# A two-layer decoder trunk: x enters transposed, TensorE multiplies zeros during the first loads, and the attention's compressed branch takes one multiply

## The chip, the cores and the metric

The kernel runs on one core of one Trainium2 chip, one execution per launch. The metric is the device time of one execution in microseconds. The engines of the core are called by the profile's names: PE (TensorE's multiplies; PEld are its weight loads), DVE (VectorE), ACT (ScalarE), POOL (GpSimd) and SP, whose queue issues most DMAs.

## What is computed

Two pre-norm residual layers over 512 positions of 1024 channels, all in float32, then a final RMSNorm. A layer runs two token mixers on one input projection (chunkwise retention, and sparse attention with compressed, selected and window branches), merges them, and adds a SwiGLU FFN of width 2816. Cut to what matters here:

```python
for i in range(2):
    h = rms_norm(x, norm_mix_g[i])               # x: (1, 512, 1024)
    proj = h @ w_in[i]                           # one projection for all branches
    q_r, k_r, v_r, g_r, q_n, kv_n, gate_n, m_a, m_b = split(proj)
    y_ret = (silu(g_r) * group_norm(retention(q_r, k_r, v_r))) @ w_o_ret[i]
    # nsa: kc, vc = compress(blocks of 32 keys/values, stride 16), an MLP with gelu
    # out = g0*softmax(q kc)vc + g1*softmax(selected) + g2*softmax(window)
    y_nsa = nsa(q_n, kv_n, gates, ...) @ w_o_nsa[i]
    x = x + (sigmoid(m_a) * y_ret + sigmoid(m_b) * y_nsa) @ w_out[i]
    x = x + (silu(a) * b) @ w_ffn_out[i]         # a, b = rms_norm(x) @ w_ffn_in[i]
return rms_norm(x, norm_final_g)
```

## The kernel before, in words

Activations are kept transposed, channels on the 128 partitions: x is eight tiles `xt` of 128 x 512. Every float32 product is made of three multiplies in a reduced format (`mm3`, lines 119 to 124): each operand is cut into a high part, a copy by ScalarE, and a low part, the residue by VectorE (`split`, line 78, for weights; `split_scaled`, line 82, for the activations `hh` and `hl`, which carry the norm's gain). A weight of 1 MB is loaded raw (`raw`, three buffers `wr`) and cut into tiles `wh` and `wl` of 1024 columns (`cut`, three buffers each). The norm's factor per position is not applied to the activations but later, to the products: `norm_stats` makes the factor `rstd`, `norm_bcast` spreads it over the partitions as `rb`.

The program is written once with tiles; a planner orders the instructions of each engine by priority (the order in which the code issues them) and by its own estimate of when inputs are ready, and adds the waits. Each engine and each DMA queue then runs its list in order. `issue_after` keeps an instruction behind another one of the same engine in that list.

Before layer 0, `setup` loads x in its natural layout (eight tiles `xnat`) and seven pieces of parameters as rows, then `setup_bias` multiplies the table of relative biases by a one-hot matrix and writes the result to DRAM (`bv`), from which eight strips per layer are loaded with shifted rows. `start_x` transposes x on PE (line 259), copies it (line 262), makes `hh` and `hl`, stores it to `xs` for the residual of layer 0, and sums the squares on VectorE (line 256).

`nsa_kv` begins each layer: the projection `psc` for the compression (48 multiplies of 512 columns), the statistics, the two key halves `psk` (24 multiplies each), the compression of keys and of values (`compress`, a generator of three steps: inputs `z`, `xa` and their cut; 2 x 16 multiplies in line 377; the gelu), the first query projection `q0` in eighteen steps, of which nine stand between two steps of the values' compression, and the values `vs` (96 multiplies of 304 columns). After it the heads run, interleaved with gate projections: scores (lines 530 to 542), transposes of the probabilities (line 573), values (lines 565, 566) and `nsa_finish` (line 588), which adds the compressed branch with two multiplies per head: the same `vc` with the high and the low half of the probabilities of a quad of heads, `pc`. Retention, output projections and FFN follow. The broadcast also stands in `hidden` (lines 871, 872), before the FFN's first products are used.

Of the kernel before, what the change touches and what calls it, by code (L numbers as in the profile page):

```python
# [14 lines left out]
P = 128  # L15
T = 512
# [15 lines left out]
class Builder:  # L32
# [100 lines left out]
    def setup(self):  # L133
        nc, a = self.nc, self.a
        self.bv = self.dr.tile([HN, 640], F32, tag="bv", name="bv")
        self.ident = self.const("ident", [P, P])
        nc.gpsimd.dma_start(self.ident, a["c_ident"])
        rows = self.u("rows", w=P)

        def load_rows():  # L140
            for l in range(DEPTH):
                nc.sync.dma_start(rows[l * 8 : l * 8 + 8], a["norm_mix_g"][l].rearrange("(k p) -> k p", p=P))
                nc.sync.dma_start(rows[16 + l * 8 : 24 + l * 8], a["norm_ffn_g"][l].rearrange("(k p) -> k p", p=P))
            nc.sync.dma_start(rows[32:40], a["norm_final_g"].rearrange("(k p) -> k p", p=P))
            nc.sync.dma_start(rows[40:72], a["cmp_pos_k"].rearrange("l (r q) d -> (l r) (q d)", q=2))
            nc.sync.dma_start(rows[72:104], a["cmp_pos_v"].rearrange("l (r q) d -> (l r) (q d)", q=2))

        self.xnat = []
        for hf in range(2):
            for t in range(NT):  # L150
                xt = self.u("xnat")
                nc.sync.dma_start(xt, a["x"][0, t * P : (t + 1) * P, hf * 512 : (hf + 1) * 512])
                self.xnat.append(xt)
            if hf == 0:
                load_rows()
        self.setup_bias()
        ps = self.tp()
        nc.tensor.transpose(ps[:, :104], rows[:104, :], self.ident[:104, :104])
        self.cols = self.const("cols", [P, 104])
        nc.vector.tensor_copy(self.cols, ps[:, :104])  # L160
# [3 lines left out]
                    "v": [self.cols[:, 72 + l * 16 : 88 + l * 16] for l in range(DEPTH)]}  # L164
        self.mhalf = self.const("mhalf", [P, NT])
# [7 lines left out]
        for g in range(2):  # L173
            nc.vector.memset(self.kcz[g].bitcast(F32), 0.0)
        self.xs = self.dr.tile([KD, P, T], F32, tag="xs", name="xs")
# [6 lines left out]
    def setup_bias(self):  # L182
# [3 lines left out]
        nc.scalar.dma_start(tab[:32], a["rel_bias"])  # L186
        nc.vector.memset(tab[32:33], NEG)
        ohv = self.u("ohv", w=256)
        nc.scalar.dma_start(ohv[:33], a["c_ohv"])
        ps = self.mm()  # L190
# [35 lines left out]
    def norm_stats(self, acc=None, ss=None):  # L226
# [8 lines left out]
        self.last_rstd = nc.gpsimd.tensor_tensor(self.rstd, var, self.mhalf, ALU.pow)  # L235

    def norm_bcast(self):
# [5 lines left out]
        for t in range(NT):  # L243
            nc.tensor.matmul(ps[:, t * P : (t + 1) * P], rep[:, t * P : (t + 1) * P], self.ident, start=True, stop=True)
        nc.scalar.activation(self.rb, ps, AF.Copy)

    def start_x(self):
        nc = self.nc
        h = []
        ss = self.small("ss", 2 * NT)  # L250
        for k in range(KD):
            if k % 4 == 0:
                for t in range(NT):
                    junk = self.u("junk")
                    xn = self.xnat[k + t]
                    nc.vector.tensor_tensor_reduce(junk, xn, xn, 1.0, 0.0, ALU.mult, ALU.add, ss[:, k + t : k + t + 1])
            ps = self.mm() if k % 2 else self.tp()
            for t in range(NT):
# [785 lines left out]
```

## Time and profile before

| | us |
|---|---|
| median of three runs | 2456.5 (2456.14 to 2457.05) |
| the profiled execution | 2455.72 |
| its span, first to last instruction | 2453.9 |
| PE busy, share of the span | 2404.7, 98% |
| DVE, ACT, POOL busy | 1409.4, 1025.3, 252.2 |
| DMA | 262.47 MB, mean 107 GB/s |

A row of a timeline gives the start and the duration of an instruction, or of several alike merged, in microseconds from the span's start; what stands in square brackets is how long the engine was idle before it and what ended that. Multiplies overlap in their records, so the pace of PE is read from the distance of two starts, not from one duration. The granted clock is the share of 2.4 GHz that TensorE was given; where nothing was recorded, the view prints 1.00, and that is so for the first 27 us.

### The profile page before, as it was taken

What the parts mean: (1) busy time and instruction counts of PE and PEld (TensorE: products, weight loads), DVE (VectorE), ACT (ScalarE), POOL (GpSimd) and SP (SyncE); (2) the same over time, 40 slices, a digit from 0 to 9 for tenths busy, and PEclk for the clock granted to TensorE, in tenths of its full rate; (3) what the DMA queues carried; (4) which work ended last, traced back from release to release, by engine and by line L of the source; (5) the groups of instructions that cost most, each with busy time, mean ns of one, the idle gap of its engine ahead of it and who ended that gap; (6) DMA issues with size and microseconds to landing.
All of it is one profiled execution on the core that took longest, in us unless ns stands there. A gap on an engine that the chain in (4) does not pass through costs nothing.

```text
span 2453.9 us, 29372 instructions
## 1 busy us (share of the span) xinstructions
PE 2404.7 (98%) x11115; PEld 1956.1 (80%) x11115; DVE 1409.4 (57%) x2797; ACT 1025.3 (42%) x1862; POOL 252.2 (10%) x225
## 2 busy tenths in 40 slices
PE   7999999999999999999989999999999999999998
PEld 5877777888888878888878787778888877888887
DVE  6778886454574633333567878864545654434334
ACT  4666675233333432222346676642333333222222
POOL 1000000010020110110110000001100202101010
PEclk9999999999999999999999999999999999999999
DMA  7523224522342432323454322235223434223221
GB/s 230 149 74 87 74 69 102 165 85 96 98 142 95 155 102 87 103 87 99 128 141 120 94 79 73 74 102 156 90 93 106 159 110 139 86 86 103 86 95 60
DMA packets 234874, 262.47 MB, mean 107 GB/s; under 512 B 42276, under 2 KB 178637, under 8 KB 234733
## 3 DMA queue, kind: packets, MB, share of 16 engines
q1 hardware_dynamic: 220720, 236.93, 32.0%
q10 hardware_dynamic: 13244, 21.41, 2.4%
q8 instruction: 87, 1.43, 0.2%
q0 software_dynamic: 768, 2.27, 0.2%
q14 instruction: 55, 0.44, 0.1%
HBM read 235.36 MB, written 25.21 MB: 106 GB/s over the span
## 4 chain that ended last, share of the span: by engine, by line
PE 89%; DVE 6%; ACT 3%; issue 1%; POOL 1%; DMA 0%; SPq 0%; POOLq 0%; ACTq 0%; DVEq 0%
PE f L123 12%; PE f L122 12%; PE f L124 12%; PE a L124 8%; PE a L123 7%; PE a L122 7%; PE o L124 7%; PE o L122 7%; PE o L123 7%; PE t L573 2%; DVE p L553 1%; PE o L566 1%; PE o L565 1%; PE a L541 1%; PE a L542 1%
## 5 line engine op out<-in xcount | busy, mean ns | idle before, releaser
L79 ACT ACTIVATE wh<-wr 128x1024 fp32r<-128x1024 f32 (+3 forms) x406 | 397.2, 980 | 986.2 <-PE f L123 263.6
L80 DVE TENSOR_TENSOR wl<-wr,wh 128x1024 fp32r<-128x1024 f32 (+3 forms) x406 | 462.7, 1143 | 220.7 <-ACT wh L79 211.9
L122 PE MATMUL f<-hh,wh 128*128 128x512 f32 x936 | 373.4, 400 | 0.7 <-ACT wh L79 0.5
L124 PE MATMUL f<-hh,wl 128*128 128x512 f32 x936 | 371.5, 397 | 1.8 <-DVE wl L80 1.7
L123 PE MATMUL f<-hl,wh 128*128 128x512 f32 x936 | 370.7, 396 | 0.1
L124 PEld LDWEIGHTS f<-hh,wl 128*128 128x128 f32 x936 | 176.7, 189 | 44.0 <-DVE wl L80 4.1
L122 PEld LDWEIGHTS f<-hh,wh 128*128 128x128 f32 x936 | 176.9, 189 | 36.4 <-ACT wh L79 1.4
L123 PEld LDWEIGHTS f<-hl,wh 128*128 128x128 f32 x936 | 176.8, 189 | 33.9 <-DVE hl L84 0.6
L523 ACT ACTIVATE p<-p,nmx 128x512 f32<-128x512 f32 (+3 forms) x256 | 142.3, 556 | 67.1 <-DVE nmx L522 65.0
L80 DVE TENSOR_TENSOR pt<-t,pt 128x512 fp32r<-128x512 f32 (+3 forms) x256 | 123.5, 485 | 56.2 <-ACT pt L79 54.6
L124 PE MATMUL a<-hh,wl 128*128 128x512 f32 x360 | 144.7, 402 | 9.3 <-DVE wl L80 9.3
L122 PE MATMUL a<-hh,wh 128*128 128x512 f32 x360 | 144.8, 402 | 0.0
L123 PE MATMUL a<-hl,wh 128*128 128x512 f32 x360 | 144.5, 401 | 0.0
L79 ACT ACTIVATE pt<-t 128x512 fp32r<-128x512 f32 (+3 forms) x256 | 109.3, 429 | 71.8 <-PE t L573 66.9
L876 POOL TENSOR_TENSOR fa<-fa,rb 128x512 f32<-128x512 f32 x44 | 77.2, 1755 | 570.1 <-ACT fa L875 570.1
L522 DVE CUSTOM_DVE_ANT_0 p<-a,strip 128x512 f32<-128x512 f32 (+3 forms) x256 | 119.5, 484 | 18.1 <-PE a L542 11.5
L122 PE MATMUL o<-hh,wh 128*128 128x512 f32 x304 | 120.1, 395 | 0.0
L124 PE MATMUL o<-hh,wl 128*128 128x512 f32 x304 | 120.0, 395 | 0.0
L123 PE MATMUL o<-hl,wh 128*128 128x512 f32 x304 | 119.9, 395 | 0.0
L573 PE MATMUL t<-ident,p 128*128 128x128 f32 x640 | 113.7, 273 | 0.0
L573 PEld LDWEIGHTS t<-ident,p 128*128 128x128 f32 x640 | 81.3, 141 | 24.3 <-issue 2.2
L565 PE MATMUL o<-pt,vs 128*128 128x512 f32 (+3 forms) x256 | 91.4, 360 | 1.4 <-ACT pt L79 1.4
(423 smaller groups left out, 4859.4 us busy)
## 6 DMA issues: line engine op xcount, KB each, us to landing
wr<-in_w_in SPq DMA_DIRECT2D x66, 1024.0 KB, 5.3
wr<-in_w_ffn_in SPq DMA_DIRECT2D x44, 1024.0 KB, 5.2
wr<-in_w_ffn_out SPq DMA_DIRECT2D x18, 1024.0 KB, 5.0
wr<-in_w_o_ret SPq DMA_DIRECT2D x16, 1024.0 KB, 5.0
wr<-in_w_in SPq DMA_DIRECT2D x36, 256.0 KB, 4.0
strip<-bv SPq DMA_DIRECT2D x32, 256.0 KB, 5.1
gs<-mt ACTq DMA_DIRECT2D x32, 256.0 KB, 2.0
wr<-in_w_o_nsa SPq DMA_DIRECT2D x16, 512.0 KB, 7.3
```

What stands on the lines that cost most here:

```text
L79: self.nc.scalar.activation(hi, src, AF.Copy)
L80: (eng or self.nc.vector).tensor_sub(lo, src, hi.bitcast(F32))
L122: self.nc.tensor.matmul(ps, lh, rh, start=start and i == 0, stop=False)
L123: self.nc.tensor.matmul(ps, lh, rl, start=False, stop=False)
L124: self.nc.tensor.matmul(ps, ll, rh, start=False, stop=stop and i == n - 1)
L522: nc.vector.tensor_tensor_reduce(p, src, self.backwards(strip, w - 1, w), -1.0, BIG, ALU.add, ALU.min, nmx[:, c])
L523: nc.scalar.activation(p, p, AF.Exp, scale=-1.0, bias=nmx[:, c], accum_out=sm[:, c])
L541: nc.tensor.matmul(ps[:, :w], qh[:, ts], ks[:, br, :w], start=True, stop=False)
L542: nc.tensor.matmul(ps[:, :w], ql[:, ts], ks[:, br, :w], start=False, stop=True)
L565: nc.tensor.matmul(po[:, j * P :], lhs, th, start=br == 0 and j == 0, stop=False)
L573: nc.tensor.transpose(pt[:, (i - j) * P : (i - j + 1) * P], pr[br][i][:, j * P : (j + 1) * P], self.ident)
L876: nc.gpsimd.tensor_mul(t, t, self.rb)
```

## The change

- The host hands over x transposed (`c_xt`) and the parameters as one 128 x 104 array of columns (`c_cols`). `setup` loads the columns; `start_x` loads two tiles of x, then the first 1 MB of `w_in`, then the other six tiles. The transposes, their copies, the sums on VectorE and the stores to `xs` are gone. `mix` of layer 0 reads the residual from `c_xt`.
- The squares of x are made by ScalarE and added by GpSimd (`acc_sq`), and `norm_stats` sums over partitions by multiplies with `ones`, as the other norms do.
- The loads for the bias table move from ScalarE's queue to GpSimd's; its multiply and its stores (`bias_rows`) move behind the first projection.
- PE issues 32 multiplies of a cleared tile, 224 columns each, at the beginning; nothing reads them.
- The statistics are in two parts: in `nsa_kv` the broadcast stands between the two key halves, and the second half is cut and multiplied ahead of the compression. The query steps are placed anew among the compression's. The broadcast is a transpose instead of a multiply by the identity.
- `vc` is one tile for both groups; `pc` holds the high half of two heads and the low half of the same two on the other 64 partitions, so that `nsa_finish` issues one multiply per head.

```diff
     def setup(self):
...
-        self.ident = self.const("ident", [P, P])
-        nc.gpsimd.dma_start(self.ident, a["c_ident"])
-        rows = self.u("rows", w=P)
...
-        self.xnat = []
-        for hf in range(2):
-            for t in range(NT):
-                xt = self.u("xnat")
-                nc.sync.dma_start(xt, a["x"][0, t * P : (t + 1) * P, hf * 512 : (hf + 1) * 512])
-                self.xnat.append(xt)
-            if hf == 0:
-                load_rows()
-        self.setup_bias()
-        ps = self.tp()
-        nc.tensor.transpose(ps[:, :104], rows[:104, :], self.ident[:104, :104])
         self.cols = self.const("cols", [P, 104])
-        nc.vector.tensor_copy(self.cols, ps[:, :104])
+        nc.sync.dma_start(self.cols, a["c_cols"])
         self.gmix = [self.cols[:, l * 8 : l * 8 + 8] for l in range(DEPTH)]
         self.gffn = [self.cols[:, 16 + l * 8 : 24 + l * 8] for l in range(DEPTH)]
...
+        self.ident = self.const("ident", [P, P])
+        nc.gpsimd.dma_start(self.ident, a["c_ident"])
+        self.setup_bias()
...
         self.kcz = [self.const(f"kcz{g}", [P, 224], F32R) for g in range(2)]
         for g in range(2):
             nc.vector.memset(self.kcz[g].bitcast(F32), 0.0)
+
+        ps = self.tp()
+        for _ in range(IDLE):
+            nc.tensor.matmul(ps[:, :224], self.kcz[0][:, :P], self.kcz[1], start=True, stop=True)
...
         nc, a = self.nc, self.a
         tab = self.u("tab", w=HN)
-        nc.scalar.dma_start(tab[:32], a["rel_bias"])
+        nc.gpsimd.dma_start(tab[:32], a["rel_bias"])
         nc.vector.memset(tab[32:33], NEG)
         ohv = self.u("ohv", w=256)
-        nc.scalar.dma_start(ohv[:33], a["c_ohv"])
-        ps = self.mm()
+        nc.gpsimd.dma_start(ohv[:33], a["c_ohv"])
+        self.bias_in = tab, ohv
+
+    def bias_rows(self):
+        nc = self.nc
+        tab, ohv = self.bias_in
+        ps = self.tp()
         nc.tensor.matmul(ps[:HN, :256], tab[:33], ohv[:33], start=True, stop=True)
...
     def norm_bcast(self):
...
         ps = self.tp()
         for t in range(NT):
-            nc.tensor.matmul(ps[:, t * P : (t + 1) * P], rep[:, t * P : (t + 1) * P], self.ident, start=True, stop=True)
+            nc.tensor.transpose(ps[:, t * P : (t + 1) * P], rep[:, t * P : (t + 1) * P], self.ident)
         nc.scalar.activation(self.rb, ps, AF.Copy)
...
     def start_x(self):
-        nc = self.nc
-        h = []
-        ss = self.small("ss", 2 * NT)
-        for k in range(KD):
-            if k % 4 == 0:
-                for t in range(NT):
-                    junk = self.u("junk")
-                    xn = self.xnat[k + t]
-                    nc.vector.tensor_tensor_reduce(junk, xn, xn, 1.0, 0.0, ALU.mult, ALU.add, ss[:, k + t : k + t + 1])
-            ps = self.mm() if k % 2 else self.tp()
...
-                nc.tensor.transpose(ps[:, t * P : (t + 1) * P], self.xnat[4 * (k // 4) + t][:, (k % 4) * P : (k % 4 + 1) * P],
-                                    self.ident)
-            xt = self.u("xt")
-            nc.scalar.activation(xt, ps, AF.Copy)
-            h.append(self.make_h(xt, self.gmix[0][:, k : k + 1]))
-            if k == 2:
-                self.first_h = self.last_hi
-            nc.gpsimd.dma_start(self.xs[k], xt)
+
+        nc = self.nc
+        xts = [self.u("xt") for _ in range(KD)]
+        w = self.a["w_in"][0][:, C_KV : C_KV + 256].rearrange("(k p) n -> p k n", p=P)
+        for k in range(2):
+            last = nc.sync.dma_start(xts[k], self.a["c_xt"][k])
+        with self.tc.issue_after(last.ins):
+            raw = self.raw([(lambda v: v, w)], KD, 256)
+        with self.tc.issue_after(self.last_load.ins):
+            for k in range(2, KD):
+                self.last_x = nc.sync.dma_start(xts[k], self.a["c_xt"][k])
+        h = [self.make_h(xts[k], self.gmix[0][:, k : k + 1]) for k in range(2)]
+        with self.tc.issue_after(self.last_hi.ins):
+            self.first_w = [self.cut(raw[:, :, j * P : (j + 1) * P]) for j in range(2)]
+        h += [self.make_h(xts[k], self.gmix[0][:, k : k + 1]) for k in range(2, KD)]
+        self.first_h = self.last_hi
         def stats():
-            s2 = self.small("s2", NT)
-            nc.vector.tensor_add(s2, ss[:, :NT], ss[:, NT:])
-            self.norm_stats(ss=s2)
-            self.norm_bcast()
-
-        self.stats = stats
+            self.bias_rows()
+            acc = None
+            for xt in xts:
+                acc = self.acc_sq(acc, xt)
+            self.norm_stats(acc)
+
+        self.stats = stats, self.norm_bcast
         return h
...
     def nsa_kv(self, l, h, q0):
...
-        if l == 0:
-            with self.tc.issue_after(self.first_h.ins):
-                wc = self.wcols(w, 0, KD, C_KV, 256)
-        else:
-            wc = self.wcols(w, 0, KD, C_KV, 256)
+        wc = self.first_w if l == 0 else self.wcols(w, 0, KD, C_KV, 256)
         psc = [self.proj_t(wc, j, h, "f") for j in range(2)]
-        wk = self.raw([(lambda v: v[:, :, :P], view(C_KV + 256, P)), (lambda v: v[:, :, P:], view(C_KV + 512, P))], KD, 256)
-        self.stats()
+        with self.tc.issue_after(self.last_x.ins) if l == 0 else nullcontext():
+            wk = self.raw([(lambda v: v[:, :, :P], view(C_KV + 256, P)), (lambda v: v[:, :, P:], view(C_KV + 512, P))], KD, 256)
+        self.stats[0]()
...
-        psk = [self.proj_t([self.cut(wk[:, :, :P])], 0, h, "a")]
+        with self.tc.issue_after(self.first_h.ins) if l == 0 else nullcontext():
+            wk = [self.cut(wk[:, :, br * P : (br + 1) * P]) for br in range(2)]
+        psk = [self.proj_t(wk, 0, h, "a")]
+        self.stats[1]()
+        psk.append(self.proj_t(wk, 1, h, "a"))
         comp = {kind: self.compress(l, kind, psc[i]) for i, kind in enumerate("kv")}
-        for kind in "kvk":
-            next(comp[kind])
-        psk.append(self.proj_t([self.cut(wk[:, :, P:])], 0, h, "a"))
+        fill = lambda n: [next(q0, None) for _ in range(n)]
+        next(comp["k"])
+        fill(9)
+        next(comp["k"])
+        next(comp["k"])
+        next(comp["v"])
         keys(0)
-        next(comp["k"])
-        for _ in range(2):
-            for _ in range(9):
-                next(q0, None)
-            next(comp["v"])
+        fill(9)
+        next(comp["v"])
+        next(comp["v"])
         keys(1)
...
-            self.vc = []
             for g in range(2):
...
-            for g in range(2):
-                vc = self.tile("cv", 2, F32R).rearrange("p (s d) -> p s d", s=4)
-                nc.gpsimd.memset(vc.bitcast(F32), 0.0)
-                for q in range(4):
-                    r = slice(32 * q, 32 * q + 32)
-                    src = po[r, g * 64 : g * 64 + 64]
-                    nc.scalar.activation(vc[r, q, :64], src, AF.Copy)
-                    nc.vector.tensor_sub(vc[r, q, 64:], src, vc[r, q, :64].bitcast(F32))
-                self.vc.append(vc)
+
+            vc = self.tile("cv", 2, F32R).rearrange("p (g e d) -> p g e d", g=2, e=2)
+            nc.gpsimd.memset(vc.bitcast(F32), 0.0)
+            src = po[:, :P].rearrange("p (g d) -> p g d", g=2)
+            for q in range(4):
+                r = slice(32 * q, 32 * q + 32)
+                nc.scalar.activation(vc[r, :, q % 2, :64], src[r], AF.Copy)
+                nc.vector.tensor_sub(vc[r, :, q % 2, 64:], src[r], vc[r, :, q % 2, :64].bitcast(F32))
+            self.vc = vc
...
-        pc += [self.u("pch", F32R), self.u("pcl", F32R)]
-        self.split(pc[0], pc[1], pt2)
+
+        for r, o in ((slice(0, 64), slice(64, P)), (slice(64, P), slice(0, 64))):
+            x = self.u("pc", F32R)
+            self.split(x[r], x[o], pt2[r])
+            pc.append(x)
...
     def nsa_finish(self, st):
...
-        for i, x in enumerate(st["pc"]):
-            nc.tensor.matmul(po, self.vc[b][:, s], x, start=False, stop=i == 1)
+        nc.tensor.matmul(po, self.vc[:, b, s % 2], st["pc"][s // 2], start=False, stop=True)
...
-                nc.vector.tensor_add(xt, ps, self.ld("xo", self.xs[n]))
+                nc.vector.tensor_add(xt, ps, self.ld("xo", self.xs[n] if l else self.a["c_xt"][n]))
...
         def stats():
             self.norm_stats(acc)
-            self.norm_bcast()
-
-        self.stats = stats
+
+        self.stats = stats, self.norm_bcast
...
                 if k0 == 0 and c == 0 and j == 0:
-                    self.stats()
+                    for part in self.stats:
+                        part()
...
+IDLE = 32
...
+def layouts(inputs):
+
+    rows = [inputs["norm_mix_g"].reshape(-1, P), inputs["norm_ffn_g"].reshape(-1, P), inputs["norm_final_g"].reshape(-1, P),
+            inputs["cmp_pos_k"].reshape(-1, P), inputs["cmp_pos_v"].reshape(-1, P)]
+    return {"c_xt": np.ascontiguousarray(inputs["x"][0].T).reshape(KD, P, T),
+            "c_cols": np.ascontiguousarray(np.concatenate([rows[0][:8], rows[0][8:], *rows[1:]]).T)}
```

## Rows read from the trace of the kernel before

**Rows 1.** Page, part 1: busy us (share of the span) and instructions of each engine.

```profile
PE 2404.7 (98%) x11115; PEld 1956.1 (80%) x11115; DVE 1409.4 (57%) x2797; ACT 1025.3 (42%) x1862; POOL 252.2 (10%) x225
```

**Rows 2.** Waits of PE, whole span: who waited for whom, us, times, longest.

```profile
PE a L124 <- DVE wl L80: 9.3, 2, 4.9
```

**Rows 3.** Timeline from the start: start us, us, engine, line, operation, count, idle before it.

```profile
0.74 1.81 SPq L152 DMA_DIRECT2D xnat<-in_x  x4
...
0.92 0.49 DVE L174 MEMSET kcz<- 128x224 f32 x2
...
8.41 4.04 SPq L91 DMA_DIRECT2D wr<-in_w_in  x3
...
16.17 1.06 ACT L79 ACTIVATE wh<-wr 128x1024 fp32r<-128x1024 f32 x1 [2.63 <-DMA wr<-in_w_in]
...
17.28 0.79 PE L122 MATMUL f<-hh,wh 128*128 128x512 f32 x1 [0.47 <-ACT wh L79]
...
20.60 0.80 PE L124 MATMUL f<-hh,wl 128*128 128x512 f32 x1 [1.67 <-DVE wl L80]
...
26.31 0.58 PE L124 MATMUL a<-hh,wl 128*128 128x512 f32 x1
```

**Rows 4.** Timeline of PE, layer 0, from the pause to the first scores.

```profile
49.17 0.79 PE L124 MATMUL a<-hh,wl 128*128 128x512 f32 x1 [4.86 <-DVE wl L80]
...
54.03 0.40 PE L123 MATMUL a<-hl,wh 128*128 128x512 f32 x1
...
56.35 0.40 PE L124 MATMUL a<-hh,wl 128*128 128x512 f32 x1
...
90.11 0.28 PE L530 MATMUL a<-ks,qh 128*128 128x256 f32 x1
```

**Rows 5.** Stretches: us, busy us of each engine, granted clock, DMA share, GB/s.

```profile
47.00:48.00 1.00, 0.00 (x0) 0.00 (x0) 1.00 (x5) 0.42 (x1) 0.00 (x0) 0.59 0.00 0
...
1263.00:1264.00 1.00, 1.00 (x3) 0.72 (x3) 0.97 (x2) 0.95 (x3) 0.00 (x0) 0.50 0.64 153
```

**Rows 6.** Timeline of PE, layer 1, from the sums to the first scores.

```profile
1242.66 0.95 PE L231 MATMUL t<-ones,sq 128*128 128x1 f32 x8
...
1247.37 1.13 PE L244 MATMUL t<-ident,rep 128*128 128x128 f32 x8 [2.72 <-DVE hrstd L289]
...
1261.74 0.50 PE L124 MATMUL a<-hh,wl 128*128 128x512 f32 x1 [4.45 <-DVE wl L80]
...
1302.02 0.28 PE L530 MATMUL a<-ks,qh 128*128 128x256 f32 x1
```

**Rows 7.** DMA issues of 0 to 10 us, then of the page: count, KB each, us to landing.

```profile
xnat<-in_x SPq DMA_DIRECT2D x8, 256.0 KB, 3.6
wr<-in_w_in SPq DMA_DIRECT2D x1, 1024.0 KB, 7.7
...
wr<-in_w_in SPq DMA_DIRECT2D x66, 1024.0 KB, 5.3
```

**Rows 8.** Lines 84, 223 (ns min/median/max), then VectorE's groups from 0 to 90 us (busy us, mean ns).

```profile
L84 DVE SCALAR_TENSOR_TENSOR hl<-xt,cols,hh x8: 732/735/751, 17.3 to 28.1; 128x512 fp32r<-128x512 f32 x8
...
L223 POOL TENSOR_TENSOR sq<-sq,sq x21: 1294/1793/1861, 829.2 to 2074.6; 128x512 f32<-128x512 f32 x21
...
L80 DVE TENSOR_TENSOR wl<-wr,wh 128x1024 fp32r<-128x1024 f32 x15 | 18.1, 1217 | 9.9 <-ACT wh L79 9.8
```

**Rows 9.** Timelines of POOL and DVE at the end of layer 0's FFN.

```profile
1224.88 1.75 POOL L223 TENSOR_TENSOR sq<-sq,sq 128x512 f32<-128x512 f32 x1 [2.90 <-ACT sq L220]
...
1225.39 1.79 DVE L84 SCALAR_TENSOR_TENSOR hl<-strip,cols,hh 128x512 fp32r<-128x512 f32 x1
```

**Rows 10.** Line 588 (ns min/median/max), then busy us of two stretches.

```profile
L588 PE MATMUL o<-pch,cv x32: 389/392/402, 144.9 to 1635.1; 128*128 128x512 f32 x32
...
36.00:90.00 54.00, 48.42 (x273) 41.61 (x272) 41.66 (x81) 33.22 (x61) 0.52 (x1) 0.94 0.52 142
90.00:440.00 350.00, 341.10 (x1727) 277.26 (x1727) 275.54 (x779) 221.77 (x527) 15.92 (x15) 1.00 0.31 86
```

More of the change, by code (lines that the diff above doesn't have):

```diff
@@ L1 @@
 import math
-from contextlib import ExitStack
+from contextlib import ExitStack, nullcontext
 import numpy as np
@@ L135, in setup @@
         self.bv = self.dr.tile([HN, 640], F32, tag="bv", name="bv")
-        self.ident = self.const("ident", [P, P])
-        nc.gpsimd.dma_start(self.ident, a["c_ident"])
-        rows = self.u("rows", w=P)
[L140 to L146, printed above, removed]
-        self.xnat = []
-        for hf in range(2):
-            for t in range(NT):
-                xt = self.u("xnat")
-                nc.sync.dma_start(xt, a["x"][0, t * P : (t + 1) * P, hf * 512 : (hf + 1) * 512])
-                self.xnat.append(xt)
-            if hf == 0:
-                load_rows()
-        self.setup_bias()
-        ps = self.tp()
-        nc.tensor.transpose(ps[:, :104], rows[:104, :], self.ident[:104, :104])
         self.cols = self.const("cols", [P, 104])
-        nc.vector.tensor_copy(self.cols, ps[:, :104])
+        nc.sync.dma_start(self.cols, a["c_cols"])
         self.gmix = [self.cols[:, l * 8 : l * 8 + 8] for l in range(DEPTH)]
@@ L234, in norm_stats @@
         nc.vector.tensor_scalar(var, ss, 1.0 / D, 1e-6, ALU.mult, ALU.add)
-        self.last_rstd = nc.gpsimd.tensor_tensor(self.rstd, var, self.mhalf, ALU.pow)
+        nc.gpsimd.tensor_tensor(self.rstd, var, self.mhalf, ALU.pow)
     def norm_bcast(self):
@@ L248, in start_x @@
         nc = self.nc
-        h = []
-        ss = self.small("ss", 2 * NT)
-        for k in range(KD):
-            if k % 4 == 0:
-                for t in range(NT):
-                    junk = self.u("junk")
-                    xn = self.xnat[k + t]
-                    nc.vector.tensor_tensor_reduce(junk, xn, xn, 1.0, 0.0, ALU.mult, ALU.add, ss[:, k + t : k + t + 1])
-            ps = self.mm() if k % 2 else self.tp()
-            for t in range(NT):
-                nc.tensor.transpose(ps[:, t * P : (t + 1) * P], self.xnat[4 * (k // 4) + t][:, (k % 4) * P : (k % 4 + 1) * P],
-                                    self.ident)
-            xt = self.u("xt")
-            nc.scalar.activation(xt, ps, AF.Copy)
-            h.append(self.make_h(xt, self.gmix[0][:, k : k + 1]))
-            if k == 2:
-                self.first_h = self.last_hi
-            nc.gpsimd.dma_start(self.xs[k], xt)
-        def stats():
-            s2 = self.small("s2", NT)
-            nc.vector.tensor_add(s2, ss[:, :NT], ss[:, NT:])
-            self.norm_stats(ss=s2)
-            self.norm_bcast()
-        self.stats = stats
+        xts = [self.u("xt") for _ in range(KD)]
[12 more added lines that the diff above has]
+        self.first_h = self.last_hi
+        def stats():
+            self.bias_rows()
[4 more added lines that the diff above has]
+        self.stats = stats, self.norm_bcast
         return h
@@ L900, in stats @@
             self.norm_stats(acc)
-            self.norm_bcast()
-        self.stats = stats
+        self.stats = stats, self.norm_bcast
         return hn
@@ L1020, in build_program @@
         Builder(tc, args, out, ctx).build()
-_INS = ["x", "norm_mix_g", "w_in", "cmp_pos_k", "cmp_pos_v", "cmp_w1_k", "cmp_w2_k", "cmp_w1_v", "cmp_w2_v",
-        "w_o_ret", "w_o_nsa", "w_out", "norm_ffn_g", "w_ffn_in", "w_ffn_out", "rel_bias", "norm_final_g"]
+_INS = ["w_in", "cmp_w1_k", "cmp_w2_k", "cmp_w1_v", "cmp_w2_v",
+        "w_o_ret", "w_o_nsa", "w_out", "w_ffn_in", "w_ffn_out", "rel_bias", "norm_final_g"]
 def kernel(**inputs):
@@ L1034 @@
     arrays.update(constants())
+    arrays.update(layouts(inputs))
     args = {}
```

## Prediction, made before any run of the changed kernel

> **What bounds the kernel now.** I read the engine totals first: TensorE (PE) is busy for nearly the whole span [rows 1]. So time is won in two ways only: by taking multiplies away in a stage where PE is never out of work, or by closing holes in PE's row. PE's waits over the whole span say where holes are: the longest sum is a weight residue (`wl`) that comes late, 9.3 us in two places of the run [rows 2]. Then I read the timelines of the two places at which a layer begins. Layer 0: the first 1 MB of `w_in` is issued on SP only behind all of x, its cut on ScalarE ends at 17.2, and the first projection multiply starts at 17.28; the third waits for its residue until 20.60, and then fourteen multiplies stand (26.31 - 20.60) / 13 = 0.44 us apart [rows 3]. Eleven later ones stand (56.35 - 54.03) / 10 = 0.23 us apart [rows 4]. 0.44 is the 1.2 GHz level, 0.23 the 2.4 GHz level: the transposes that PE did before them had not brought the clock up. In the middle of the stage PE stands for 4.86 us [rows 4], the granted clock falls in that pause [rows 5], and the eleven multiplies from 49.17 again go at the slow pace. The attention scores (line 530) begin at 90.11 [rows 4]. Layer 1 has the same stage with two holes, 2.72 and 4.45 us, and a halved clock behind each [rows 5, 6].
>
> **The first weights (layer 0).** Removed: eight natural-layout loads, seven small loads, 32 transposes of x plus one of the parameters, their eight copies on ScalarE, eight sums on VectorE and eight stores on GpSimd's queue. SP issues the columns, two tiles of x and then `w_in`: with x loads at 0.45 us each (four in 1.81) the 1 MB is issued at about 2.0, not at 8.41. Its landing has no row of its own. Behind 1 MB of x it took 7.7 us, the median 1 MB load of this matrix takes 5.3 [rows 7]: 9.7 or 7.3. About 0.56 MB stands ahead of it, so I take 8.2. The cut costs 1.06 [rows 3], so the first multiply starts at 9.3 (8.4 to 10.8) instead of 17.28: 8.0 us. The two tiles of x land 3.6 us after their issue [rows 7], before the weights, and their high and low parts are made meanwhile. The other six tiles land behind `w_in`; each step of eight needs one low part of 0.74 us on VectorE [rows 8] and gives PE six multiplies, 1.4 us, so after the first two steps PE is the slower one.
>
> **The zeros.** 32 multiplies of 224 columns at the slow pace: 32 x 0.44 x 224 / 512 = 6.1 us, from about 1.5, when `kcz` is cleared [rows 3], to 7.6. They cost nothing: PE has nothing else until 9.3. If the weights came at the early bound, 8.4, they would still be done. What they give: if the clock is up when the real work starts, fourteen multiplies save 14 x 0.21 = 2.9 us. No multiply by nothing but zeros is in this trace, so the bound is 0 to 2.9; I take 2.9, since what raised the clock in layer 0 were the fourteen and the eleven multiplies themselves, one on the other [rows 3, 4], and the zeros are issued like these.
>
> **Rest of the stage, layer 0.** From first multiply to scores takes 90.11 - 17.28 = 72.8 us now. Of this goes: the start gap (two multiplies in 3.3 us become a wait of about 1.2 for one residue [rows 8]), 1.6; the slow start, 2.9; the wait of 4.86, since the second key half is now cut and multiplied before the compression's many VectorE steps and no longer queued behind them; the slow multiplies after it, 11 x 0.21 = 2.3; and half of the norm's broadcast, 0.5 (eight records in 1.13 us [rows 6] become four as transposes). Sum 12.2. Added on PE: the sums of squares through `ones`, 0.95 [rows 6], and the bias multiply, which was hidden in the start and now stands in the stream, about 1. The scores would start at 9.3 + 72.8 - 12.2 + 1.95 = 71.9, 18.2 us earlier, if no new hole opened. One will: the row scale `rb` now depends on a chain of eight squares and seven GpSimd additions of 1.79 us [rows 8], 12.6 us, which begins when the last tiles are there (about 15) and with the steps behind it ends near 33; PE has 96 multiplies, 22 us, from 9.3, so it is covered to about 34 and by nine steps of the query projection to 40. But VectorE, busy for 41.7 of the 54 us from 36 to 90 [rows 10], must do nearly all of that work in the 39 us from 33 to 72, and weights are cut only three tiles ahead. I charge 5 us (0 to 12). Layer 0: 13 us (6 to 18).
>
> **Layer 1.** From line 231 at 1242.66 to the scores at 1302.02 [rows 6]. The broadcast is moved behind the first 24 key multiplies (5.6 us), longer than the 4.7 us that its inputs take, so 2.72 goes; 4.45 goes as above; with them eight slow multiplies behind each, 2 x 8 x 0.21 = 3.3; half the broadcast, 0.5. Sum 11. The same packed VectorE work is charged with 3.5 (0 to 9): 7.5 us (2 to 11).
>
> **Attention.** `nsa_finish` issues one multiply per head instead of two: 32 of the 64 go, each 0.23 us of PE's pace: 7.4 us. The stage is PE's: 341 of 350 us busy, ScalarE 222, VectorE 276 [rows 10], so I take it whole (5 to 7.5). The split behind it becomes two halves on 64 partitions, one more step of some 0.7 us on either engine per quad, eight quads; the values' fewer pieces give part of it back. PE's work around it covers that; without cover it would cost 5.
>
> **Small things.** The other two broadcasts stand in PE's row before the FFN: 2 x 0.5 = 1. The residual of layer 0 is read from the input, the same size. The stores removed only free DMA.
>
> Sum: 13 + 7.5 + 7.4 + 1 = 29 us. The profiled execution took 2455.7 (span 2453.9 and 1.8 around it), 0.8 below the median; 2455.7 - 29 + 0.8 = 2427.5, so 2427.
>
> **A rule beside a row.** The statistics move from VectorE to GpSimd, which a page speaks against. The rows: an addition takes 1.29 to 1.86 us there, median 1.79, and a low part on VectorE that falls into one takes 1.79 instead of 0.74 [rows 8, 9]. The Trainium skill's page "GPSIMD Engine Reference", section 4.1, puts two-input elementwise work on GpSimd at about twice VectorE's time; an estimate from that is 7 x 1.5 = 10.3 us for the chain and an `rb` 2.3 us earlier than by the rows. The measurement decides here, and the sum uses 1.79.
>
> **The rivals.** (1) The statistics become the bound of layer 0. If PE's order has the `ones` multiplies behind the 48 of the first projection, PE stands from about 22 until the additions end, 28 or 29, and the clock falls in the pause: 6.5 + 2.3 = 9 us; six low parts of x that meet additions cost VectorE up to 6 x 1.05 us more. For it: the planner has misjudged this chain already (2.72 in layer 1 [rows 6]). Against it: then 24 key multiplies stood ready and were drawn forward. The layer-0 gain falls to 2 to 6 and the total to some 16: 2440. (2) The zeros do not carry the clock over to 9.3, or the weights come so late that it falls again: 2.9 us less, 2430. (3) Slower: SP's order. The eight strip loads need `bv`, which is now written behind the bias multiply and, on GpSimd's queue, among the additions; compression weights queued behind the strips on SP would wait for it. Each microsecond that these weights come after PE asks for them (about 40) is one lost; it turns the sign only past the 34 us that the rest gains at most, that is with `bv` landing after some 65. GpSimd's chain ends near 30, so this is unlikely. (4) No new hole at all: 18 + 11 + 7.4 + 1 = 37.5, 2418.5.
>
> **How the numbers follow.** Forecast with its charges (a gain of 20 to 35) 0.62; rival 1, 0.22; rival 2, 0.08; rival 4, 0.05; rival 3, 0.03. The range takes in rival 4 and, on the other side, rival 1 with layer 1 at its poorer end: 2417 to 2443. About 0.2%, 5 us, is what a measurement of this kernel can tell from no change; every case but the third lies beyond it, save a poor end of rival 1: faster 0.95, same 0.02, slower 0.03.
>
> **What would show it.** Right: the first `w_in` multiply near 9 at a pace of 0.23; no wait of `wl` of more than 3 us in either stage; the broadcast of layer 1 without a wait; scores at about 77 in layer 0; line 588's successor with 32 records. Wrong: PE waiting on line 231 or for a GpSimd sum before 35 (rival 1), a pace of 0.44 after 9 (rival 2), SP waiting for `bv` with PE waiting for weights (rival 3).

## The result, and the profile after

The changed kernel took 2429.2 us (median of four runs, 2427.0 to 2430.4), the kernel before 2456.3 on the same chip: ratio 0.989, 95% interval 0.987 to 0.991. The forecast was 2427 with a range of 2417 to 2443. The profiled execution took 2427.0, with a span of 2425.2 against 2453.9: 28.7 us. The time came out as forecast, but not for the reasons forecast. Only about 12 of these 28.7 us are the change's own work; the other 17 come from a thing that is not in the sum at all.

The page, engine totals of the changed kernel (as [rows 1]), and under it the largest waits of PE over the whole span (as [rows 2]: who waited for whom, us in all, times, longest):

```profile
PE 2377.0 (98%) x11074; PEld 1945.8 (80%) x11074; DVE 1413.5 (58%) x2779; ACT 1029.9 (42%) x1862; POOL 258.3 (11%) x224
```

```profile
PE o L366 <- DVE pt L80: 6.1, 2, 3.1
PE o L557 <- DVE pt L80: 6.0, 6, 1.7
PE o L366 <- DVE wl L80: 5.6, 6, 2.0
PE a L532 <- DVE nmx L513: 4.2, 4, 1.4
PE t L233 <- DVE rep L229: 4.0, 3, 2.4
```

The 9.3 us for a weight residue of the keys are gone. In their place PE waits for the parts of the compression (line 366, 6.1 and 5.6) and for the row scale (line 233). PE's busy time fell by 27.7 us, although PE has only 41 records fewer (what was added set against what went); that is the first sign that something other than removed work is at play.

The landing of the first weights (DMA issues of 0 to 20 us, as [rows 7]) and the timelines of the start (start us, us, engine, line, operation, count, idle before it), as [rows 3, 4]:

```profile
wr<-in_w_in SPq DMA_DIRECT2D x1, 1024.0 KB, 6.9
```

```profile
2.12 0.43 SPq L91 DMA_DIRECT2D wr<-in_w_in  x1
...
9.09 2.01 ACT L79 ACTIVATE wh<-wr 128x1024 fp32r<-128x1024 f32 x2 [2.23 <-DMA wr<-in_w_in]
...
1.53 5.87 PE L158 MATMUL t<-kcz,kcz 128*128 128x224 f32 x32 [1.53 <-DVE kcz L154]
8.37 0.59 PE L180 MATMUL t<-ohv,tab 33*16 33x256 f32 x2 [0.97 <-DMA ohv<-c_ohv]
10.20 0.50 PE L122 MATMUL f<-hh,wh 128*128 128x512 f32 x1 [1.24 <-ACT wh L79]
...
29.61 1.05 PE L220 MATMUL t<-ones,sq 128*128 128x1 f32 x8
...
34.37 1.11 PE L233 MATMUL t<-ident,rep 128*128 128x128 f32 x4 [2.43 <-DVE rep L229]
...
60.45 0.58 PE L366 MATMUL o<-wh,pt 128*128 128x256 f32 x1 [3.08 <-DVE pt L80]
...
64.75 0.58 PE L366 MATMUL o<-wl,pt 128*128 128x256 f32 x1 [2.01 <-DVE wl L80]
...
85.45 0.28 PE L521 MATMUL a<-ks,qh 128*128 128x256 f32 x1
```

The weights are issued at 2.12 and multiplied from 10.20, as forecast within 1 us. But the scores begin at 85.45, not at 77: three new pauses stand between (2.43, 3.08 and 2.01). Two stretches behind them (us, busy us of PE with the count of multiplies, granted clock, DMA share, GB/s) have the halved clock:

```profile
36.00:38.00 2.00, 2.00 (x6) 0.50 0.00 0
...
66.00:68.00 2.00, 2.00 (x11) 0.50 0.98 294
```

Layer 1, the timeline that answers to [rows 6]: the broadcast (line 233) has no wait any more, yet the stage from the sums to the scores is only 1.1 us shorter (58.21 for 59.36), since the same two pauses of line 366 stand in it:

```profile
1225.90 0.95 PE L220 MATMUL t<-ones,sq 128*128 128x1 f32 x8
...
1232.29 0.60 PE L233 MATMUL t<-ident,rep 128*128 128x128 f32 x4
...
1259.16 0.58 PE L366 MATMUL o<-wh,pt 128*128 128x256 f32 x1 [3.06 <-DVE pt L80]
...
1263.45 0.58 PE L366 MATMUL o<-wl,pt 128*128 128x256 f32 x1 [2.01 <-DVE wl L80]
...
1284.11 0.28 PE L521 MATMUL a<-ks,qh 128*128 128x256 f32 x1
```

The finish of the attention, line 578, has 32 records; the row of line 588 in [rows 10] is one of two sets of 32:

```profile
L578 PE MATMUL o<-pc,cv x32: 388/392/396, 139.9 to 1614.3; 128*128 128x512 f32 x32
```

Where, then, did the time go? I cut both timelines at the first multiply of each stage. The middle column is the first experiment, explained below.

| us | before | changed, weights where before had them | changed |
|---|---|---|---|
| to the first projection multiply | 17.3 | 10.0 | 10.2 |
| to the scores, layer 0 | 72.8 | 75.4 | 75.3 |
| attention, layer 0 | 337.2 | 334.8 | 335.0 |
| retention, layer 0 | 388.4 | 388.3 | 385.4 |
| mix and FFN, layer 0 | 427.0 | 426.3 | 420.0 |
| to the scores, layer 1 | 59.4 | 58.5 | 58.2 |
| attention, layer 1 | 337.1 | 334.8 | 334.0 |
| retention, layer 1 | 388.3 | 388.3 | 383.8 |
| mix and last FFN | 420.0 | 419.3 | 416.8 |
| sum | 2447.4 | 2435.7 | 2418.7 |

Retention, mix and FFN, whose code the change leaves nearly as it was, became 17.7 us shorter (1623.7 to 1606.0); the two shorter broadcasts are 1 us of it. One stretch inside the first FFN, in which PE never stands in either kernel, shows it: 330 us hold 1422 multiplies before and 1443 after, at the same granted clock, 232.1 and 228.7 ns each.

Stretch of the FFN, the kernel before, then the changed one:

```profile
880.00:1210.00 330.00, 330.00 (x1422) 1.00 0.29 95
```

```profile
880.00:1210.00 330.00, 330.00 (x1443) 1.00 0.32 102
```

### The profile page after: what moved, and what is told of

Same layout as the page of the kernel before. It is cut to its first block, busy times and chain, and to the rows that moved or that the text cites. A ratio compares the mean times of both kernels' runs of the same rounds, so it can differ in the third digit from the quotient of the medians.

```text
span 2425.2 us, 29236 instructions
## 1 busy us (share of the span) xinstructions
PE 2377.0 (98%) x11074; PEld 1945.8 (80%) x11074; DVE 1413.5 (58%) x2779; ACT 1029.9 (42%) x1862; POOL 258.3 (11%) x224
## 4 chain that ended last, share of the span: by engine, by line
PE 89%; DVE 6%; ACT 3%; issue 1%; POOL 1%; DMA 0%; SPq 0%; POOLq 0%; ACTq 0%; DVEq 0%
PE f L123 11%; PE f L122 11%; PE f L124 11%; PE a L123 8%; PE a L122 8%; PE o L123 8%; PE a L124 8%; PE o L122 8%; PE o L124 7%; PE t L564 2%; DVE p L544 1%; PE o L557 1%; PE o L556 1%; PE a L532 1%; PE a L533 1%
## 5 line engine op out<-in xcount | busy, mean ns | idle before, releaser
L79 ACT ACTIVATE pt<-t 128x512 fp32r<-128x512 f32 (+3 forms) x256 | 109.1, 429 | 75.7 <-PE t L564 72.9
L123 PE MATMUL a<-hl,wh 128*128 128x512 f32 x336 | 133.1, 396 | 0.0
L122 PE MATMUL a<-hh,wh 128*128 128x512 f32 x336 | 133.0, 396 | 0.0
L124 PE MATMUL a<-hh,wl 128*128 128x512 f32 x336 | 131.9, 392 | 0.0
L123 PE MATMUL o<-hl,wh 128*128 128x512 f32 x328 | 129.3, 394 | 0.0
L122 PE MATMUL o<-hh,wh 128*128 128x512 f32 x328 | 128.9, 393 | 0.0
L124 PE MATMUL o<-hh,wl 128*128 128x512 f32 x328 | 127.9, 390 | 0.0
```

Source lines behind the costliest of these rows:

```text
L79: self.nc.scalar.activation(hi, src, AF.Copy)
L122: self.nc.tensor.matmul(ps, lh, rh, start=start and i == 0, stop=False)
L123: self.nc.tensor.matmul(ps, lh, rl, start=False, stop=False)
L124: self.nc.tensor.matmul(ps, ll, rh, start=False, stop=stop and i == n - 1)
```

## The experiments

**Where the weights lie.** The change drops one small value of the start (a ring of six buffers, 192 bytes), and everything allocated behind it moves down. The weight tiles, the last in the memory, began at offset 288 from a multiple of 512 bytes in every partition and now begin at 96; the moving tiles stay at 416. (These addresses are those of the built programs; no trace shows them.) The accumulator banks are dealt out in another order too, so I moved the weights alone, in either kernel.

Changed kernel, weights back at 288:

```diff
-        var = self.small("var", NT)
+        var = self.small("var", NT, bufs=12)
```

> The changed kernel with one small ring given six more buffers (192 bytes), so that every weight tile in the on-chip memory lies at the address it had in the kernel before (offset 288 from a multiple of 512 bytes); no instruction differs. Theory 'placement' (the pace of 512-column multiplies follows where the weight tiles lie): the pace of the layers' multiplies goes back from 230.2 to 232.4 ns in every stage, about 8,500 multiplies x 2.2 ns = 18 us, 2447 us (2444 to 2450). Rival 'banks or order' (the pace follows the accumulator banks, which are dealt out otherwise, or the start's zeros, or the chip of the run): 2429 us and 230.2 ns, as the changed kernel.

Kernel before, weights at 96:

```diff
-            s2 = self.small("s2", NT)
+            s2 = self.small("var", NT)
```

> The kernel before with one small value of its start taken from a ring that is there already, so that a ring of 192 bytes falls away and every weight tile lies where the changed kernel has it (offset 96 from a multiple of 512 bytes); no instruction differs. Theory 'placement': pace 230.2 ns instead of 232.4 in every stage, 2456 - 18 = 2438 us (2435 to 2441). Rival 'banks or order': 2456 us, 232.4 ns.

Changed kernel, weights at 416 (the first diff with bufs=16):

> The changed kernel with the weight tiles 320 bytes higher, at offset 416 from a multiple of 512 bytes, the offset that the moving tiles have and that the few weights of the retention's own product have (227.9 ns in both kernels). Theory 'placement', as those few rows read: 227.9 ns where the weights are weight tiles, 7,000 x 1.6 ns = 11 us less, 2418 us (2414 to 2424). Rival 'banks or order': 2429 us.

Measured: 2443.9, 2436.4 and 2406.6 us, the kernel before 2457.0 beside them; ratios 0.995 (0.993 to 0.997), 0.992 (0.990 to 0.993), 0.980 (0.978 to 0.981). The same stretch of the FFN in the three:

```profile
880.00:1210.00 330.00, 330.00 (x1422) 1.00 0.30 96
```

```profile
880.00:1210.00 330.00, 330.00 (x1443) 1.00 0.31 100
```

```profile
880.00:1210.00 330.00, 330.00 (x1457) 1.00 0.34 107
```

The count follows the offset and not the kernel: 1422 at 288 and 1443 at 96, in both. At 416 it is 1457, 226.5 ns each, and 22.6 us less than the change as it is, twice the 11 us that were expected. In each of these runs the trace has PE's multiplies in the same order as its parent's, one by one. So the rival of banks and order falls. Then the pairs of offsets by themselves, with nothing else at work:

```diff
+    for mo in MOFF:
+        for wo in WOFF:
...
+                hi, lo = (wt[:, w0 + b + k * P : w0 + b + k * P + P] for b in (0, 1152))
+                mh, ml = (mv[:, m0 + b : m0 + b + 512] for b in (k % 2 * 1024, 512 + k % 2 * 1024))
+                nc.tensor.matmul(p, hi, mh, start=k == 0, stop=False)
+                nc.tensor.matmul(p, hi, ml, start=False, stop=False)
+                nc.tensor.matmul(p, lo, mh, start=False, stop=k == 7)
```

> Leaves the whole computation out: only series of 24 multiplies of 512 columns on constants, in the kernel's pattern (high by high, low by high, high by low), for 16 offsets of the weights by 8 offsets of the moving tile, and no other engine at work. Theory 'placement': the spacing within a series differs with the offsets by 1 to 5 ns around 230 and repeats the pairs seen in the two kernels (weights 416 and moving 416: 228; 288 and 416: 232.5; 96 and 416: 229.5). Rival 'placement through a collision with other engines' memory traffic': one spacing for all pairs.

The offsets are again those of the addresses (the tiles of the series begin 128 bytes above a multiple of 512). The first of the 128 series went at the slow clock and is left out. Mean spacing of consecutive 512-column multiplies, ns; the kernels' figures are for their weight tiles, or, swapped, for weight tiles that are streamed:

```
moving offset, weights offset   series alone   in the kernels
416, 288                        233.7          232.6  (before)
416,  96                        229.7          229.5  (changed)
416, 416                        227.5          226.8  (weights at 416)
288, 416                        233.0          232.6  (before, swapped)
lowest and highest of 127 pairs 227.3, 234.7
```

Over these pairs the spacing lies between 227.3 and 234.7 ns, and pairs that differ only by 256 bytes in the moving offset agree within 0.2 ns. The kernels' figures come in the same order, within about 1 ns. The difference needs no other engine, so a collision with other engines' traffic falls too. Why certain pairs are slow (the load of the weights, or the stream beside it) was not tried.

Last of this set, the kernel before with its weights at 416 (the ring of the first diff with bufs=10):

> The kernel before with one small ring given four more buffers (128 bytes), so that its weight tiles lie at offset 416 from a multiple of 512 bytes instead of 288; no instruction differs. Theory 'placement is a term of its own, independent of the change': the pace goes from 232.4 to 226.8 ns and the time falls as the changed kernel's did between the same two offsets (2443.9 to 2406.6, 37 us): 2419 us, less than the changed kernel as it is. Rival 'only the changed kernel can use it' (the kernel before is held up by other engines in more places): a fall of 10 to 25 us, 2431 to 2446 us.

2413.4 us, ratio 0.983 (0.981 to 0.984): 128 unused bytes in the old kernel give 42 us, more than the whole change, and no less than the 37 us of the changed kernel. Its stretch of the FFN:

```profile
880.00:1210.00 330.00, 330.00 (x1458) 1.00 0.33 106
```

At equal offsets the change itself is worth 13.0 us (288), 7.2 (96) and 6.7 (416), each with 4 to 6 us of uncertainty, where the sum had 29.

**The zeros.**

```diff
-IDLE = 32
+IDLE = 0
```

> The changed kernel without its 32 multiplies of zeros, all else and the placement of the weights the same. Theory of the prediction: the first fourteen projection multiplies go at the 1.2 GHz level (0.44 us each instead of 0.23), 14 x 0.21 = 2.9 us, and all of it reaches the end: 2432 us. Rival 'the statistics bound this stage': the time up to the broadcast is set by the chain of squares and additions, TensorE waits 2.4 us for it at 34.4, and the slow start is taken out of that wait: at most 0.5 us, 2429.5 us.

2427.7 us, ratio 0.989 (0.987 to 0.990): no difference. Timeline of the start without them, and the stretch behind the broadcast:

```profile
11.30 0.63 PE L123 MATMUL f<-hl,wh 128*128 128x512 f32 x1
...
14.69 0.63 PE L124 MATMUL f<-hh,wl 128*128 128x512 f32 x1
...
35.53 0.66 PE L233 MATMUL t<-ident,rep 128*128 128x128 f32 x4 [1.80 <-DVE rep L229]
```

```profile
36.00:38.00 2.00, 2.00 (x11) 1.00 0.00 0
```

The first multiplies are slow, as forecast (seven steps in 3.39 us), about 2 us in all, and they began 0.5 us later (10.71). But of these 2.5 us the broadcast is only 1.2 later, since the rest is taken out of the wait for `rep`, and after that shorter wait the clock stays up, where the changed kernel's fell. The scores come at 84.76, 0.7 us earlier than with the zeros. Nor do the zeros always hold the clock. Eight profiles here have 32 zeros; in two (the changed kernel, and with the weights at 288) all the first multiplies go at the fast level, in six they or those right behind them go at the slow one. With the doubled finish (below), for one:

```profile
10.28 0.79 PE L122 MATMUL f<-hh,wh 128*128 128x512 f32 x1 [2.27 <-ACT wh L79]
```

**The statistics.** The additions on VectorE instead of GpSimd:

```diff
-                acc = self.acc_sq(acc, xt)
+                acc = self.acc_sq(acc, xt, nc.vector)
```

> The changed kernel with the seven additions of squares at the start on VectorE instead of GpSimd, all else and the placement the same. Theory 'the statistics bound the stage': the additions (11.35 us on GpSimd) are done some 5 us earlier, the broadcast no longer waits (2.4 us) and no slow multiplies follow it (about 12 x 0.2 us), the scores come 3 to 6 us earlier, 2424 to 2426 us. Rival 'VectorE's work behind the row scale bounds it': the holes later in the stage (3.08 and 2.01 us, at 60 and 65) grow by what is won before, 2428 to 2430 us.

2423.8 us, ratio 0.987 (0.986 to 0.989), so 5.4 less in the medians than the change as it is. The intervals of the two ratios overlap, so the total alone can hardly tell them apart; the stage can, below. VectorE's timeline has six of the seven additions in 4.65 us, GpSimd's in the changed kernel all seven in 11.35:

```profile
19.00 4.65 DVE L212 TENSOR_TENSOR sq<-sq,sq 128x512 f32<-128x512 f32 x6
```

```profile
18.21 11.35 POOL L212 TENSOR_TENSOR sq<-sq,sq 128x512 f32<-128x512 f32 x7
```

PE's timeline with the additions on VectorE: the wait for `rep` is 1.29 at 31.88; the pauses of line 366 stay, 3.10 and 2.72.

```profile
31.88 0.66 PE L233 MATMUL t<-ident,rep 128*128 128x128 f32 x4 [1.29 <-DVE rep L229]
...
58.80 0.39 PE L366 MATMUL o<-wh,pt 128*128 128x256 f32 x1 [3.10 <-DVE pt L80]
...
63.10 0.58 PE L366 MATMUL o<-wl,pt 128*128 128x256 f32 x1 [2.72 <-DVE wl L80]
```

Behind that shorter wait the multiplies go on at the fast pace. From first multiply to scores the stage takes 72.1 us instead of 75.3, although this start had slow multiplies and the changed kernel's had none. The statistics do bound the first half of the stage. The second pause grew by 0.7: a little of the rival is true as well.

The clearing of the compression's tiles on GpSimd fell on the same moment as the row scale on VectorE; I made it small:

```diff
-            nc.gpsimd.memset(xa, 0.0)
+            nc.gpsimd.memset(xv[:, :, :, NCMP:], 0.0)
```

> The changed kernel with GpSimd clearing only the one column in 32 that is not written otherwise, instead of the whole 256-column tile, in both compressions; placement the same. Theory 'collision': the row-scale steps on VectorE (hrstd 2.02, rep 2.21 us) no longer stand beside eight clearings on GpSimd and take 0.1 and 0.6 to 0.7, the wait for the broadcast falls from 2.43 to about 0.9, and with it part of the slow multiplies: 1.5 to 3.5 us less, 2426 to 2428 us. Rival 'VectorE's later work bounds the stage': the later holes grow by as much, 2429 us.

2424.5 us, ratio 0.987 (0.986 to 0.989). The total alone can't be told from the changed kernel here either. VectorE and GpSimd in the changed kernel, then both with the small clearing, and PE's wait there:

```profile
32.02 2.02 DVE L273 TENSOR_SCALAR hrstd<-rstd 128x4 f32<-128x4 f32 x1 [1.16 <-POOL rstd L224]
32.10 2.21 DVE L229 COPY rep<-rstd 128x512 f32<-128x512 f32 x1
...
31.95 2.07 POOL L348 MEMSET xa<- 128x256 f32 x8
```

```profile
35.79 0.31 DVE L273 TENSOR_SCALAR hrstd<-rstd 128x4 f32<-128x4 f32 x1 [1.15 <-POOL rstd L224]
35.87 0.49 DVE L229 COPY rep<-rstd 128x512 f32<-128x512 f32 x1
...
35.72 0.35 POOL L348 MEMSET xa<- 128x8 f32 x8
...
36.42 0.66 PE L233 MATMUL t<-ident,rep 128*128 128x128 f32 x4 [0.70 <-DVE rep L229]
```

A write of 4 columns took 2.02 us beside the eight whole clearings, and ended as they did, at 34.0; beside the eight small ones it took 0.31. PE's wait for `rep` fell from 2.43 to 0.70 and the clock stayed up, although the first multiply came 1.7 us later in this profile (11.86). The stage takes 73.1 us instead of 75.3. The pause for `wl` grew from 2.01 to 3.00.

**The order of the compressions.**

```diff
         next(comp["k"])
+        next(comp["v"])
         fill(9)
         next(comp["k"])
         next(comp["k"])
-        next(comp["v"])
```

> The changed kernel with the first step of the compression of the values issued directly behind that of the keys, ahead of the query projection, in both layers; nothing added or removed, placement the same. Theory 'order': the wait for its operand (3.1 us in each layer, at 60.4 and 1259.2) and the slow multiplies behind it go, 3 to 5 us a layer, 2420 to 2424 us. Rival 'VectorE is packed': the same work only delays the weight residues and the query's parts, a wait of the same size stands elsewhere in the stage, 2428 to 2431 us.

2419.2 us, ratio 0.985 (0.984 to 0.987), 10 less in the medians. PE's timeline in layer 0 and in layer 1:

```profile
52.24 0.58 PE L366 MATMUL o<-wl,p 128*128 128x256 f32 x1 [4.34 <-DVE wl L80]
...
1244.32 0.38 PE L366 MATMUL o<-wl,p 128*128 128x256 f32 x1 [1.41 <-DVE wl L80]
...
1246.84 0.39 PE L366 MATMUL o<-wl,p 128*128 128x256 f32 x1 [1.35 <-DVE wl L80]
```

The wait for `pt` is gone in both layers. In layer 1 two waits of 1.4 replace 3.06 and 2.01 and the stage takes 53.5 us instead of 58.2. In layer 0 a wait of 4.34 for a weight residue of the keys' compression stands in its place, as the rival had it; its stage is 2.4 shorter (72.9). The two stages thus show 7.1 of the 10.

**The finish of the attention**, undone:

```diff
-        nc.tensor.matmul(po, self.vc[:, b, s % 2], st["pc"][s // 2], start=False, stop=True)
+        for i, x in enumerate(st["pc"]):
+            nc.tensor.matmul(po, self.vc[b][:, s], x, start=False, stop=i == 1)
```

> The changed kernel with two multiplies per head in the finish of the attention, as the kernel before has it (values of the compressed branch in two tiles, probabilities in a high and a low tile), all else and the placement the same. Theory of the prediction: 32 multiplies x 0.23 = 7.4 us more, 2437 us. Rival 'partly beside the path' (the attention of the changed kernel was 2.3 us a layer shorter than before at equal placement): 4.6 us more, 2434 us.

2431.0 us, ratio 0.990 (0.989 to 0.992), which alone can't be told from the changed kernel. The stage can: from the scores to the end of the attention 336.7 and 336.2 us (86.42 to 423.14 and 1284.87 to 1621.04), with the single finish 335.0 and 334.0. That is 1.7 and 2.2 us, 3.9 in all, instead of 7.4. In layer 1 the 16 multiplies are worth 3.7 by their own spacing; of that the projection multiplies between which they stood take back 1.1 and the multiplies by the values 1.1, each summed over its steps from start to start. PE's waits in that stage come to much the same (6.9 us, doubled 6.5), so most of it is not a longer wait; what it is stays open.

**Together**: weights at 416, additions on VectorE, values first, small clearings; then the same with 52 zeros (IDLE = 52).

> The changed kernel with the weights at offset 416, the additions of the start on VectorE, the compression of the values first and the small clearings. If the four add up as measured or expected one by one: 2406.6 - 5 - 10 - 2 = 2390 us (2386 to 2394). Rival 'two of them close the same holes': 2396 to 2400 us.

> As the kernel with the four together, with 52 multiplies of zeros instead of 32, so that they end near 9.5 instead of 7.4 and the pause before the first weights is short. Theory 'the zeros pay once the statistics no longer bound the start': no slow multiplies at the start in any profile (0 to 10 of them, 0.2 us each, with 32), 1 to 2 us less than with 32. Rival: the same time as with 32, as without zeros it was the same.

2395.7 us (2391.0 to 2396.8) and 2395.6 (2395.2 to 2397.7), ratios 0.975 and 0.976. Beside the changed kernel with its weights at 416 (2406.6) the three edits give 10.9, as the rival had it, not the 20 that the medians gave one by one (5.4, 4.7 and 10.0). The stages gave 3.2, 2.1 and 7.1 one by one, 12.4, which leaves little for it; so it is not shown that the edits close partly the same holes. The medians one by one may have been too large. In the profile of the first, which is of its fastest run, PE's timeline has no pause of over 1.4 us in layer 0 and the scores come at 75.28:

```profile
43.05 0.38 PE L366 MATMUL o<-wl,p 128*128 128x256 f32 x1 [1.37 <-DVE wl L80]
...
75.28 0.28 PE L521 MATMUL a<-ks,qh 128*128 128x256 f32 x1
```

In that of the second they come at 81.55, with one wait of 4.49 for such a residue, at 49.41. Its first multiplies all go at the fast level, so the 52 zeros do hold the clock, and the time is the same. But this pair does not test the zeros alone: with them the planner ordered VectorE and SP otherwise too (VectorE makes a weight residue of the keys at 41.78 in the first, ahead of the last two parts of the values; in the second it makes the one that PE waits for at 48.14, behind them all). So it shows that this program is no faster, and not that more zeros bring nothing.

## Why the forecast held, and where its steps failed

- **First weights (8.0): right.** 7.1 in the profile. The landing took 6.9 us, between the two bounds of [rows 7]; over the profiles of its variants the first multiply came between 9.8 and 11.9.
- **Zeros (2.9): wrong at the end of the path.** In the changed kernel's profile they do what they should (a pace of 0.23 from the first multiply), but the time is waited away at 34.37. Without them the kernel takes the same. And rival 2, that they do not carry the clock over, was held at 0.08 but shows in six of the eight profiles with 32 zeros; it cost nothing that could be measured, for the same reason.
- **Rest of layer 0: mis-sized.** Each wait that was to go went. The charge for new holes was 5 (0 to 12); the holes are 2.43, 3.08 and 2.01, and beside them PE works at half the clock for 6 us (34 to 40) and some 7.5 (61 to 71), half of which is lost: 7.5 + 6.8 = 14.3. The sum had 67.6 us from first multiply to scores; 67.6 - 5 + 14.3, less 1 for the bias multiply below, is 75.9, and 75.3 was measured, where before had 72.8. Two steps failed. "Covered to about 34" counted all 96 multiplies of the first projection and the keys, but the broadcast stands ahead of the last nine: PE was through with the others at 31.9, and `rep` was ready at 34.3 (forecast: near 33), some 1.7 us of that by the collision with the clearings, which no term had. This is rival 1's kind of hole, worth 2.4 and 3 us here where rival 1 had 9. The other holes are the charge's own kind, VectorE behind the row scale: 5.1 and 3.8 us, 8.9 instead of 5. The charge did not price the clock behind a wait: after the first two it was at 0.50, and behind the third it still was. The gain to the scores is 4.7 instead of 13, within the 2 to 6 of rival 1, which I held less likely; but its details did not come. The `ones` multiplies stood behind 34 key multiplies and waited for nothing, and the low parts of x kept their 0.74 us.
- **The bias multiply (1 us added): wrong.** It stands at 8.37, in the gap before the weights, and costs nothing.
- **Layer 1 (7.5, at least 2): mis-sized**, 0.8 at equal offsets by the table (288), and 2.0 and 1.7 with the weights of both kernels at 96 and at 416. 2.72 and 4.45 went as forecast; 3.06 and 2.01 came for them. The charge of 3.5 (0 to 9) had to be 9 to 10. That the order, not VectorE's mass of work alone, made this hole is shown: the same work with the values first takes 4.7 us less.
- **Attention (7.4, at least 5): mis-sized**, 4.6 at equal offsets by the table (3.2 at 96 and at 416), 3.9 by undoing it. "The stage is PE's, so I take it whole" is the step that failed: the multiplies are gone at their full price, and others of the stage took part of it back. Why is not shown.
- **FFN broadcasts (1): right**, 0.5 in each FFN.
- **The rule on GpSimd: right.** The Trainium skill's "GPSIMD Engine Reference", section 4.1, keeps two-input additions off GpSimd. Here the trace agrees: they took 1.62 us each there and 0.78 on VectorE, and the move back gave 3.2 us in the stage and 5.4 in the medians. On GpSimd the chain of seven took 11.35 us, between the 10.3 that I had estimated from that section and the 12.6 by the rows.
- **Rival 3 did not show**: the strips' loads were issued from 21.27 and no PE wait hangs on them.
- **What was not in the sum: 17 us** from 192 bytes. The change's own terms, about 12 us in place of 29, give 2444 (as the run with the weights back at 288 did), just outside the range; the offset brought the time back to the forecast. The forecast was right in its number by luck, by two errors of like size.
- **A slip in a sum**: rival 4's 18 + 11 + 7.4 + 1 gives 2419.1, not 2418.5; nothing hangs on it.

## What to carry to other kernels

Before the parts of a change are priced, compare the pace of a stage that it does not touch: the count of multiplies in a stretch in which PE never stands. If it differs, look at what moved in the memory, and measure every edit at equal addresses; the best offset is a search of its own, worth more here than the change. Judge a small edit by the stage that it touches as well as by the total: here single edits of 2 to 5 us could hardly be told from noise in the total. And where a stage has several chains that end close together, a removed wait is worth only the distance to the next one; price a remaining pause with the slow multiplies behind it.

## What the runs showed that was not expected

- A 512-column multiply takes 226.5 to 232.1 ns in one and the same stage of this kernel (227.3 to 234.7 in the series alone) by the offsets of weights and moving tile alone, with the granted clock at 1.00 throughout: 42 us of 2456.
- A VectorE step of 4 columns took 2.02 us beside a train of GpSimd clearings, 0.31 beside a train of small ones.
- After a pause of 1.80 us (35.53, without zeros) the granted clock stayed at 1.00; after 2.43 (34.37, with zeros) it was 0.50. In the second the pause ended 1.2 us earlier and cost more.
